# A decoder layer's Mamba mixer: its output kept channel-major, two heads per array pass, z as stationary weights

## The chip, the cores and the metric

The kernel runs on one core of a Trainium2 chip. The metric is device time in microseconds of one launch, the median of three runs; the profile is one further execution of the same program. TensorE multiplies (PE for the products, PEld for the loads of their stationary operand), VectorE (DVE), ScalarE (ACT) and GpSimd (POOL) do the element-wise work, and SyncE (SP) issues most transfers. Each engine takes its instructions strictly in program order; semaphores hold an instruction until its operands are there.

## The reference, cut to what matters

A trunk of two layers over 256 tokens of width 2048: a Mamba-2 layer, a gated feed-forward network, a shared K/V projection, an attention layer, and a second feed-forward network. The change lies in the Mamba-2 mixer alone (batch 1, 64 heads of 64 channels, 8 groups of 512 channels, state 128, two chunks of 128 tokens):

```python
def mamba2_mixer(x, w_in, conv_w, conv_b, dt_bias, a_log, d_skip, norm_w, w_out):
    zxbcdt = x @ w_in
    z, xbc, dt = ...                      # 4096, 4096 + 2*8*128, 64 columns
    xbc = silu(causal_dwconv(xbc, conv_w, conv_b))
    xs, b_ssm, c_ssm = ...
    dt = softplus(dt + dt_bias)
    a = -exp(a_log)
    y = ssd_chunked(xs * dt[..., None], a * dt, b_ssm, c_ssm)
    y = y + d_skip[:, None] * xs
    y = y.reshape(Bsz, S, D_INNER) * silu(z)
    yg = y.reshape(Bsz, S, N_SSM_GROUPS, D_INNER // N_SSM_GROUPS)
    yg = yg * rsqrt(mean(square(yg), axis=-1, keepdims=True) + RMS_EPS)
    return (yg.reshape(Bsz, S, D_INNER) * norm_w) @ w_out

def ssd_chunked(xdt, adt, b, c):          # chunks of l = 128 tokens
    a_cum = cumsum(a, axis=2)
    decay_in = exp(where(causal, a_cum[l] - a_cum[s], -inf))
    cb = einsum('bclgn,bcsgn->bclsg', c, b)
    y_diag = einsum('bclsgr,bcsgrp->bclgrp', cb[..., None] * decay_in, x)
    decay_to_end = exp(a_cum[:, :, -1:] - a_cum)
    chunk_states = einsum('bclgn,bclgr,bclgrp->bcgrpn', b, decay_to_end, x)
    ...                                   # prev: the state before each chunk
    y_off = einsum('bclgn,bcgrpn,bclgr->bclgrp', c, prev, exp(a_cum))
    return y_diag + y_off
```

With two chunks only the second has a state before it, so the kernel works `y_off` out once per group, as a product of the 128 x 128 block C2·B1 (`bc`) with the first chunk's scaled inputs (`xe`).

## The kernel before

**Weights as a stream of steps.** Every large product is cut into chunks of 512 weight columns (`chunks`, L59) and these into steps of 512 KB (`cut`, L81), 882 in all. A step's weights are loaded into a `raw` tile by SP (`load`, L162, four buffers), and `split` (L172) makes of them a rounded part `hi` (ACT, L183) and a remainder `lo` (DVE, L184). The activations are kept the same way, as `hi` and `lo` in `hT` (the layer's input, transposed), `yT` (the mixer's output, transposed) and others. A product is then the sum of three in the format fp32r: hi·hi, hi·lo and lo·hi. `splits` (L188) writes the split of step i+3 into the middle of step i, with four `hi` and four `lo` buffers, so weights are split up to three steps ahead; ACT can write a `hi` buffer only when TensorE has finished the step that used it four steps before.

**Two ways to multiply.** In mode "X" (`half`, L196) the activations are stationary and 512 weight columns stream past: 12 products of 128 x 512 a step (L206, L207, L211), and the result has tokens on the partitions. In mode "W" (`whole`, L225) the weights are stationary and the activations stream: 8 products of 128 x 512 (`hi` weights, both parts of the activations at once, L243) and 8 of 128 x 256 (`lo` weights, L245) a step, and the result has channels on the partitions, in two halves that are summed on the way out (`gather`, L546: a copy on ACT, an addition on DVE). An odd step of a mode-W chunk takes its `lo` products first (L233).

**What stands around the products.** `products(i)` writes step i; the functions registered with `at(i, f)` are written right behind it (L1059 to L1062). So the order of all engines' work is fixed by these step numbers. Accumulators come from `acc_pair` (three pairs of PSUM banks in turn), everything else that TensorE writes from `tp_tile` (two banks in turn).

**A group of the mixer.** For each of the 8 groups there are 8 steps for x (mode W) and 8 for z (mode X), 16 in all; `s0` is the first. In this text "step 7" of a group is s0+7, and what is planned at s0+16 and later stands in the next group's steps 0 and up. By step, in the plan at L775 to L797:
- 3: `m_load` fetches the group's cumulated decays, for all 8 heads, broadcast over the partitions (`mA`, two tiles, POOL's queue).
- 6: `m_cb` multiplies B and C (L673, L674; plain float32, which the trace shows as two passes each), DVE masks the result (`cb`, L676), ACT copies `bc` (L680). 6 to 8: `m_decay` (DVE, L685, L686) and `m_exp` (ACT, L690) make exp(a_cum[l] - a_cum[s]).
- 4 and 8: the gathers of x; 5 and 9: the four taps of the convolution (`taps`, L570: ACT L573, DVE L578). 12: `x_silu`. 13, 14: `m_mask` (DVE, L694) multiplies `cb` in.
- 15: `x_turn` transposes x to token-major (8 transposes, L708) and ACT copies it out (L709). 16: `x_dt` scales by dt and D (DVE, L716 to L719); `z_silu` (ACT).
- 18 and 19: `y_off` (one float32 product of 128 x 512, L732) and `y_diag` (8 float32 products a chunk, each with one head's 128 x 128 decay block stationary and its 64 channels moving, L724); DVE adds them up (L727, L734, L735).
- 21 to 23: `z_gate` (DVE, L744; ACT squares and sums, L747), `z_rms` (DVE L751, POOL L752), `z_scale` (DVE, L757).
- 28, 29: `z_turn` transposes the result back to channel-major, 4 transposes each (L340), and writes `yT` as `hi` (ACT, L763) and `lo` (DVE, L765).

Before the groups, `dt_turn` (L643) turns the per-head rows of dt, a_cum and their exponentials into `aux`. After them the product with `mamba_w_out` (mode X) reads `yT`.

Of the kernel before, what the change touches and what calls it, by code (L numbers as in the profile page):

```python
# [24 lines left out]
P = 128  # L25
# [16 lines left out]
NEG = -1.0e30  # L42


COL_AT, N_COL = {}, 0
for _name, _n in (("cw", 4 * CONV), ("cb", CONV), ("nw", DI), ("fw0", 6 * DFF), ("fcb0", 2 * DFF), ("fw1", 6 * DFF),
                  ("fcb1", 2 * DFF), ("dtb", P), ("alog", P), ("d", NH * P)):
    COL_AT[_name] = N_COL
    N_COL += _n // P
# [9 lines left out]
def chunks():  # L59
# [14 lines left out]
    for g in range(NG):  # L74
        out += some("W", "mamba_w_in", 0, DI + g * NC, 1, KD) + some("X", "mamba_w_in", 0, z + g * NC, 1, KD)
# [15 lines left out]
def yoco_kernel(ctx: ExitStack, tc: tile.TileContext, x, lmg, lmb, lfg, lfb, x_t, columns, w, out):  # L91
# [22 lines left out]
    cols = base.tile([P, N_COL], F32, name="cols")  # L114

    def load_cols():
        nc.sync.dma_start(cols, columns)
# [424 lines left out]
    d_bc = cols[:, COL_AT["d"]:COL_AT["d"] + NH]  # L542
    acum_d = dram.tile([NH, S], F32, name="acum_d")
    aux = mp.tile([P, 6, NH], F32, name="aux")
# [52 lines left out]
    def dt_exp():  # L597

        an = T["an"] = mp.tile([NH, 1], F32, name="an")
# [31 lines left out]
    def dt_cum():  # L631
# [9 lines left out]
        nc.scalar.activation(ex[:, P:], ac[:, P:], AF.Exp)  # L641

    def dt_turn():  # L643
        u, e, q, r, dt, ac, ex = T["t"]
        pt = tp_tile()
        for i, (t, c) in enumerate(((dt, 0), (dt, 1), (ac, 0), (ac, 1), (ex, 0), (ex, 1))):
            nc.tensor.transpose(pt[:, i * NH:(i + 1) * NH], t[:, c * P:(c + 1) * P], ident[:NH, :NH])
        nc.vector.tensor_copy(aux, pt[:, :6 * NH].rearrange("p (a h) -> p a h", h=NH))
# [38 lines left out]

    def m_exp(g, c):
# [14 lines left out]
    def x_turn(g):  # L703
        G[g]["xs"] = xs = t4k("xs")
        for h in range(2):
            ps = tp_tile()
            for i in range(4):
                nc.tensor.transpose(ps[:, i * P:(i + 1) * P], G[g]["xc"][:, i, h * P:(h + 1) * P], ident)  # L708
            nc.scalar.copy(xs[:, h], ps)  # L709

    def x_dt(g):
        xs = G[g]["xs"]
        G[g]["xdt"] = xd = t4k("xdt")
        G[g]["xe"] = xe = mp.tile([P, NC], F32, tag="xe", name="xe", bufs=1)
        for h in range(2):
            nc.vector.tensor_mul(heads(xd[:, h]), heads(xs[:, h]), hd(aux[:, h], g))  # L716
        nc.vector.tensor_mul(heads(xe), heads(xd[:, 0]), hd(aux[:, 4], g))
        for h in range(2):
            nc.vector.tensor_mul(heads(xs[:, h]), heads(xs[:, h]), hd(d_bc, g))  # L719

    def y_diag(g, c):
        ps = tp_tile()
        for h in range(8):
            nc.tensor.matmul(ps[:, h * 64:(h + 1) * 64], G[g]["A", c][:, h, :],  # L724
                             G[g]["xdt"][:, c, h * 64:(h + 1) * 64], start=True, stop=True)
        y = G[g]["xs"]
# [373 lines left out]
```

## Time and profile before

| what | value |
|---|---|
| median of three runs | 2558.22 us (2558.15 to 2558.3) |
| the profiled execution's own time | 2558.33 us |
| its span, first to last instruction | 2556.4 us |
| granted TensorE clock, mean | 0.999 |
| one group of the mixer, in the steady part | 51.02 us |
| the eight groups, from 154 to 563 us | 409 us, of which DVE 313 busy, ACT 228 |

A row of the timeline is: start, duration of the whole row, engine, line, operation, what it writes and reads, shape, how many in a row, and in brackets the idle time before it with what ended it. Durations of TensorE's products are modelled and overlap, so its pace is read from one start to the next. A row of the waits is: who waited for whom, the total, how often, the longest. A row of the chain in order of time is: start, duration, what. A row of the groups is: line, engine, operation, shape and count, then busy time and mean duration in ns.

### The profile page before, as it was taken

What the parts mean: (1) busy time and instruction counts of PE and PEld (TensorE: products, weight loads), DVE (VectorE), ACT (ScalarE), POOL (GpSimd) and SP (SyncE); (2) the same over time, 40 slices, a digit from 0 to 9 for tenths busy, and PEclk for the clock granted to TensorE, in tenths of its full rate; (3) what the DMA queues carried; (4) which work ended last, traced back from release to release, by engine and by line L of the source; (5) the groups of instructions that cost most, each with busy time, mean ns of one, the idle gap of its engine ahead of it and who ended that gap; (6) DMA issues with size and microseconds to landing.
All of it is one profiled execution on the core that took longest, in us unless ns stands there. A gap on an engine that the chain in (4) does not pass through costs nothing.

```text
span 2556.4 us, 35404 instructions
## 1 busy us (share of the span) xinstructions
PE 2543.6 (99%) x13744; PEld 2199.0 (86%) x13744; DVE 1666.5 (65%) x2138; ACT 1300.0 (51%) x1634; POOL 72.3 (3%) x87
## 2 busy tenths in 40 slices
PE   9999999999999999999999999999999999999998
PEld 8888888888888888888888888888888888888887
DVE  6877788854676666666444745655777676765545
ACT  6656556633465555555333444543555555554333
POOL 0000000000200000000000200000200000000001
PEclk9999999999999999999999999999999999999999
DMA  7555555557566565666676655456665666566675
GB/s 260 197 186 188 189 179 186 192 186 234 185 228 190 187 190 184 194 192 190 199 229 199 222 190 173 157 173 223 222 197 187 192 186 192 185 195 200 198 224 163
DMA packets 141495, 500.98 MB, mean 196 GB/s; under 512 B 15616, under 2 KB 16128, under 8 KB 141328
## 3 DMA queue, kind: packets, MB, share of 16 engines
q1 hardware_dynamic: 136976, 483.46, 58.8%
q0 software_dynamic: 4064, 14.75, 1.8%
q8 instruction: 107, 1.75, 0.3%
q14 instruction: 60, 0.49, 0.1%
q10 hardware_dynamic: 288, 0.52, 0.1%
HBM read 490.22 MB, written 8.45 MB: 195 GB/s over the span
## 4 chain that ended last, share of the span: by engine, by line
PE 98%; DVE 1%; issue 0%; ACT 0%; DMA 0%; SPq 0%; DVEq 0%
PE acc L243 36%; PE acc L245 19%; PE acc L211 13%; PE acc L206 13%; PE acc L207 13%; PE tp L724 1%; PE tp L211 0%; PE tp L207 0%; PE tp L206 0%; DVE lo L184 0%; PE tp L340 0%; PE tp L708 0%; PE tp L965 0%; PE tp L732 0%; DVE r L417 0%
## 5 line engine op out<-in xcount | busy, mean ns | idle before, releaser
L184 DVE TENSOR_TENSOR lo<-raw,hi 128x1024 fp32r<-128x1024 f32 (+1 forms) x871 | 1063.2, 1226 | 732.2 <-ACT hi L183 728.3
L183 ACT CAST hi<-raw 128x1024 fp32r<-128x1024 f32 (+1 forms) x871 | 912.6, 1049 | 915.6 <-PE acc L211 377.4
L243 PE MATMUL acc<-hT,hi 128*128 128x512 f32 x3984 | 961.4, 392 | 0.4 <-ACT hi L183 0.4
L243 PEld LDWEIGHTS acc<-hT,hi 128*128 128x128 f32 x3984 | 731.0, 188 | 141.7 <-ACT hi L183 1.0
L245 PEld LDWEIGHTS acc<-hT,lo 128*128 128x128 f32 x3984 | 512.5, 191 | 20.0
L245 PE MATMUL acc<-hT,lo 128*128 128x256 f32 x3984 | 522.5, 283 | 0.0
L207 PE MATMUL acc<-lo,gT 128*128 128x512 f32 (+1 forms) x678 | 254.5, 378 | 0.0
L206 PE MATMUL acc<-hi,gT 128*128 128x512 f32 (+1 forms) x678 | 254.1, 377 | 0.0
L211 PE MATMUL acc<-hi,gT 128*128 128x512 f32 (+1 forms) x678 | 200.8, 377 | 0.0
L206 PE MATMUL acc<-hi,hT 128*128 128x512 f32 x448 | 179.9, 402 | 0.0
L207 PE MATMUL acc<-lo,hT 128*128 128x512 f32 x448 | 175.2, 391 | 0.0
L207 PEld LDWEIGHTS acc<-lo,gT 128*128 128x128 f32 x678 | 127.7, 188 | 23.4
L206 PEld LDWEIGHTS acc<-hi,gT 128*128 128x128 f32 x678 | 127.5, 188 | 23.0
L211 PEld LDWEIGHTS acc<-hi,gT 128*128 128x128 f32 x678 | 124.9, 188 | 23.7
L211 PE MATMUL acc<-hi,hT 128*128 128x512 f32 x448 | 139.4, 392 | 0.6 <-DVE hT L353 0.6
L211 PEld LDWEIGHTS acc<-hi,hT 128*128 128x128 f32 x448 | 83.4, 188 | 20.5 <-DVE hT L353 3.0
L206 PEld LDWEIGHTS acc<-hi,hT 128*128 128x128 f32 x448 | 84.2, 188 | 17.2 <-ACT hT L352 1.3
L206 PE MATMUL acc<-hi,yT 128*128 128x512 f32 (+1 forms) x270 | 98.9, 371 | 0.0
L207 PEld LDWEIGHTS acc<-lo,hT 128*128 128x128 f32 x448 | 84.3, 188 | 16.9 <-DVE lo L184 0.9
L207 PE MATMUL acc<-lo,yT 128*128 128x512 f32 (+1 forms) x270 | 98.6, 369 | 0.0
L211 PE MATMUL acc<-hi,yT 128*128 128x512 f32 (+1 forms) x270 | 77.7, 369 | 0.0
L578 DVE SCALAR_TENSOR_TENSOR g<-u,cols,g 128x254 f32<-128x254 f32 (+1 forms) x176 | 73.5, 478 | 5.3 <-ACT g L573 5.3
(200 smaller groups left out, 1875.6 us busy)
## 6 DMA issues: line engine op xcount, KB each, us to landing
raw<-in_w SPq DMA_DIRECT2D x881, 512.0 KB, 4.1
mA<-acum_d POOLq DMA_DIRECT2D x16, 512.0 KB, 5.2
hres<-r POOLq DMA_DIRECT2D x12, 512.0 KB, 6.3
r<-hres SPq DMA_DIRECT2D x12, 512.0 KB, 5.1
r<-in_x SPq DMA_DIRECT2D x4, 512.0 KB, 5.2
gb<-in_ln_mix_g SPq DMA_DIRECT2D x8, 256.0 KB, 6.0
gb<-in_ln_mix_b SPq DMA_DIRECT2D x8, 256.0 KB, 6.4
gb<-in_ln_ffn_g SPq DMA_DIRECT2D x8, 256.0 KB, 5.5
```

What stands on the lines that cost most here:

```text
L183: nc.scalar.copy(h[:, sl], t[:, sl])
L184: nc.vector.tensor_sub(l[:, sl], t[:, sl], h[:, sl].bitcast(F32))
L206: nc.tensor.matmul(a, th, h[:, kk, sl], start=k == 0, stop=False)
L207: nc.tensor.matmul(a, th, l[:, kk, sl], start=False, stop=False)
L211: nc.tensor.matmul(a, ch.x.lo(k)[:, ts], h[:, kk, sl], start=False, stop=k == ch.nk - 1)
L243: nc.tensor.matmul(banks[j], h[:, kk, js], ch.x.both(k), start=begins, stop=ends, skip_group_check=True)
L245: nc.tensor.matmul(banks[j][:, :S], l[:, kk, js], ch.x.hi(k), start=begins, stop=ends, skip_group_check=True)
L578: nc.vector.scalar_tensor_tensor(d, u[:, i % 2, :S - k], c1(self.at_w, w[n - 1 - k] + self.ia + i), d, op0=OP.mult, op1=OP.add)
L724: nc.tensor.matmul(ps[:, h * 64:(h + 1) * 64], G[g]["A", c][:, h, :], G[g]["xdt"][:, c, h * 64:(h + 1) * 64], start=True, stop=True)
```

## The change

Channels stay on the partitions from the convolution to `yT`:
- z is computed in mode W like x, so it arrives as channels by tokens, in two halves, and is gathered, then put through silu (`z_silu`, by halves at steps 12 and 16).
- `y_diag` has the moving and the stationary operand exchanged: a head's 64 columns of `xdt` are stationary, its 128 x 128 decay block moves, and two heads go to the two halves of the array's columns (`tile_position`); the 16 products of a group write one accumulator pair. `y_off` becomes four products, with `xe` stationary and `bc` moving. The second chunk's decay factor exp(a_cum) is taken from `mA` (`m_into`, two exponentials on 64 partitions each, ACT) instead of from `aux`.
- D·x is a scaled copy in channel-major form (`y_d`, four on ACT).
- The squares are summed over the group's channels by two additions on DVE (`z_sum`) and two products with a column of 1/512 (`z_rms`); the root is spread over the partitions by a diagonal (`z_diag`, DVE) and one product with a matrix of ones (`z_scale`); then DVE multiplies and the `hi` and `lo` of `yT` follow. The transposes back (`z_turn`) go.
- TensorE's small float32 work stands at three places of a group, steps 6, 13 and 18 (= 2 of the next), instead of six: `z_rms` with `m_cb`, the preceding group's `z_scale` with `x_turn`, and `y_off` with `y_diag`.
- D is passed with one value per channel (32 columns instead of 64), and `cols`, `an` and the new `mean` are padded to a multiple of 64 floats.

```diff
+LINE = 64
...
-                  ("fcb1", 2 * DFF), ("dtb", P), ("alog", P), ("d", NH * P)):
+                  ("fcb1", 2 * DFF), ("dtb", P), ("alog", P), ("d", DI)):
...
     for g in range(NG):
-        out += some("W", "mamba_w_in", 0, DI + g * NC, 1, KD) + some("X", "mamba_w_in", 0, z + g * NC, 1, KD)
+        out += some("W", "mamba_w_in", 0, DI + g * NC, 1, KD) + some("W", "mamba_w_in", 0, z + g * NC, 1, KD)
...
-    cols = base.tile([P, N_COL], F32, name="cols")
+    cols = base.tile([P, -(-N_COL // LINE) * LINE], F32, name="cols")
...
     def load_cols():
-        nc.sync.dma_start(cols, columns)
+        nc.sync.dma_start(cols[:, :N_COL], columns)
...
     def c1(name, j):
...
-    d_bc = cols[:, COL_AT["d"]:COL_AT["d"] + NH]
+    mean = base.tile([P, LINE], F32, name="mean")
+    nc.gpsimd.memset(mean, 1.0 / NC)
+    ones = base.tile([P, P], F32, name="ones")
+    nc.gpsimd.memset(ones, 1.0)
...
-    aux = mp.tile([P, 6, NH], F32, name="aux")
+    aux = mp.tile([P, 5, NH], F32, name="aux")
...
     def gather(ch, half, dst, scale=None):
...
     def dt_exp():
...
-        an = T["an"] = mp.tile([NH, 1], F32, name="an")
+        an = T["an"] = mp.tile([NH, LINE], F32, name="an")[:, :1]
...
-        nc.scalar.activation(ex[:, P:], ac[:, P:], AF.Exp)
...
     def dt_turn():
...
-        for i, (t, c) in enumerate(((dt, 0), (dt, 1), (ac, 0), (ac, 1), (ex, 0), (ex, 1))):
+        for i, (t, c) in enumerate(((dt, 0), (dt, 1), (ac, 0), (ac, 1), (ex, 0))):
...
-        nc.vector.tensor_copy(aux, pt[:, :6 * NH].rearrange("p (a h) -> p a h", h=NH))
+        nc.vector.tensor_copy(aux, pt[:, :5 * NH].rearrange("p (a h) -> p a h", h=NH))
...
     def bc_silu(dst, g0):
...
+    def m_into(g):
+        G[g]["eA"] = e = mp.tile([P, 4, P], F32, tag="eA", name="eA", bufs=1)
+        for q in range(2):
+            ps = slice(64 * q, 64 * q + 64)
+            nc.scalar.activation(e[ps], G[g]["A", 1][ps].rearrange("p (j q) l -> p j q l", q=2)[:, :, q, :], AF.Exp)
     def m_exp(g, c):
...
     def x_turn(g):
-        G[g]["xs"] = xs = t4k("xs")
-        for h in range(2):
-            ps = tp_tile()
-            for i in range(4):
-                nc.tensor.transpose(ps[:, i * P:(i + 1) * P], G[g]["xc"][:, i, h * P:(h + 1) * P], ident)
-            nc.scalar.copy(xs[:, h], ps)
-    def x_dt(g):
-        xs = G[g]["xs"]
...
+        ps = acc_pair()
...
-            nc.vector.tensor_mul(heads(xd[:, h]), heads(xs[:, h]), hd(aux[:, h], g))
+            for i in range(4):
+                nc.tensor.transpose(ps[:, h, i * P:(i + 1) * P], G[g]["xc"][:, i, h * P:(h + 1) * P], ident)
+        for h in range(2):
+            nc.vector.tensor_mul(heads(xd[:, h]), heads(ps[:, h]), hd(aux[:, h], g))
...
+    def y_d(g):
+        G[g]["y"] = y = t4k("y").rearrange("p a (k t) -> p (a k) t", t=S)
+        for i in range(4):
+            nc.scalar.activation(y[:, i, :], G[g]["xc"][:, i, :], AF.Copy, scale=c1("d", 4 * g + i))
+    def y_diag(g):
+        ps = acc_pair()
+        for c in range(2):
+            for h in range(8):
+                j, q = divmod(h, 2)
+                nc.tensor.matmul(ps[64 * q:64 * q + 64, c, j * P:(j + 1) * P], G[g]["xdt"][:, c, h * 64:(h + 1) * 64],
+                                 G[g]["A", c][:, h, :], start=True, stop=True, tile_position=(0, 64 * q))
+        y = G[g]["y"].rearrange("p j (c l) -> p c j l", c=2)
+        nc.vector.tensor_add(y, y, ps.rearrange("p c (j l) -> p c j l", l=P))
+    def y_off(g):
+        ps = tp_tile()
+        for j in range(4):
+            nc.tensor.matmul(ps[:, j * P:(j + 1) * P], G[g]["xe"][:, j * P:(j + 1) * P], G[g]["bc"], start=True,
+                             stop=True)
+        e, y = G[g]["eA"], G[g]["y"][:, :, P:]
+        nc.vector.tensor_mul(e, e, ps.rearrange("p (j l) -> p j l", l=P))
+        nc.vector.tensor_add(y, y, e)
+    def z_silu(g, half):
+        if half == 0:
+            G[g]["sz"] = t4k("sz").rearrange("p a (k t) -> p (a k) t", t=S)
+        sz = G[g]["sz"][:, 2 * half:2 * half + 2, :]
+        gather(chZ[g], half, sz)
+        nc.scalar.activation(sz, sz, AF.Silu)
+    def z_gate(g):
+        y, sz = G[g]["y"], G[g]["sz"]
+        nc.vector.tensor_mul(y, y, sz)
+        nc.scalar.activation(sz, y, AF.Square)
+    def z_sum(g):
+        sz = G[g]["sz"]
+        nc.vector.tensor_add(sz[:, :2], sz[:, :2], sz[:, 2:])
+        nc.vector.tensor_add(sz[:, 0], sz[:, 0], sz[:, 1])
+    def z_rms(g):
+        ps = tp_tile()
...
-            nc.vector.tensor_mul(heads(xs[:, h]), heads(xs[:, h]), hd(d_bc, g))
-    def y_diag(g, c):
+            nc.tensor.matmul(ps[:, h:h + 1], G[g]["sz"][:, 0, h * P:(h + 1) * P], mean[:, :1], start=True, stop=True)
+        rr = mp.tile([P, 2, 1], F32, tag="rr", name="rr")
+        nc.vector.tensor_scalar(rr[:, :, 0], ps[:, :2], RMS_EPS, None, op0=OP.add)
+        nc.gpsimd.tensor_tensor(rr, rr, mhalf, op=OP.pow)
+        G[g]["rr"] = rr
+    def z_diag(g):
+        G[g]["rd"] = rd = mp.tile([P, 2, P], F32, tag="rd", name="rd", bufs=1)
+        for h in range(2):
+            nc.vector.tensor_scalar(rd[:, h], ident, G[g]["rr"][:, h, :], None, op0=OP.mult)
+    def z_scale(g):
...
-        for h in range(8):
-            nc.tensor.matmul(ps[:, h * 64:(h + 1) * 64], G[g]["A", c][:, h, :],
-                             G[g]["xdt"][:, c, h * 64:(h + 1) * 64], start=True, stop=True)
-        y = G[g]["xs"]
-        nc.vector.tensor_add(y[:, c], y[:, c], ps)
-    def y_off(g):
-        ps = tp_tile()
-        nc.tensor.matmul(ps, G[g]["bc"], G[g]["xe"], start=True, stop=True)
-        y, xe = G[g]["xs"], G[g]["xe"]
-        nc.vector.tensor_mul(heads(xe), heads(ps), hd(aux[:, 5], g))
-        nc.vector.tensor_add(y[:, 1], y[:, 1], xe)
-    def z_silu(g):
-        G[g]["sz"] = sz = t4k("sz")
-        for h in range(2):
-            nc.scalar.activation(sz[:, h], chZ[g].part[h], AF.Silu)
-    def z_gate(g):
-        y, sz = G[g]["xs"], G[g]["sz"]
-        nc.vector.tensor_mul(y, y, sz)
-        G[g]["ss"] = ss = mp.tile([P, 2, 1], F32, tag="ss", name="ss")
-        for h in range(2):
-            nc.scalar.activation(sz[:, h], y[:, h], AF.Square, accum_out=ss[:, h, :])
-    def z_rms(g):
-        G[g]["rr"] = rr = mp.tile([P, 2, 1], F32, tag="rr", name="rr")
-        nc.vector.tensor_scalar(rr, G[g]["ss"], 1.0 / NC, RMS_EPS, op0=OP.mult, op1=OP.add)
-        nc.gpsimd.tensor_tensor(rr, rr, mhalf, op=OP.pow)
-    def z_scale(g):
-        y = G[g]["xs"]
-        for h in range(2):
-            nc.vector.tensor_scalar(y[:, h], y[:, h], G[g]["rr"][:, h, :], None, op0=OP.mult)
-    def z_turn(g, p):
-        ps = turn_pair([G[g]["xs"]], p)
-        ks = [(4 * g + 2 * p + kk, ps[:, kk * S:(kk + 1) * S]) for kk in range(2)]
-        for k, s in ks:
-            nc.scalar.activation(yT[:, k, 0, :], s, AF.Identity, scale=c1("nw", k))
-        for k, s in ks:
-            nc.vector.scalar_tensor_tensor(yT[:, k, 1, :], s, c1("nw", k), yT[:, k, 0, :].bitcast(F32),
-                                           op0=OP.mult, op1=OP.subtract)
+        nc.tensor.matmul(ps[:, :S], ones, G[g]["rd"].rearrange("p h t -> p (h t)"), start=True, stop=True)
+        y = G[g]["y"]
+        for i in range(4):
+            nc.vector.scalar_tensor_tensor(y[:, i, :], y[:, i, :], c1("nw", 4 * g + i), ps[:, :S], op0=OP.mult,
+                                           op1=OP.mult)
+        hi, lo = (yT[:, 4 * g:4 * g + 4, a, :] for a in range(2))
+        nc.scalar.copy(hi, y)
+        nc.vector.tensor_sub(lo, y, hi.bitcast(F32))
...
         s0 = chX[g].first
...
+        at(s0 + 6, m_into, g)
...
         conv4(chX[g], 4 * g, lambda g=g: x_new(g), 0).plan()
-        at(s0 + 12, x_silu, g)
+        at(s0 + 11, x_silu, g)
...
-        at(s0 + 15, x_turn, g)
-        at(s0 + 16, x_dt, g)
-        at(s0 + 16, z_silu, g)
+        if g:
+            at(s0 + 13, z_scale, g - 1)
+        at(s0 + 13, x_turn, g)
+        at(s0 + 13, y_d, g)
+        for b in range(2):
+            at(chZ[g].ready(b), z_silu, g, b)
...
-        at(s0 + 18, y_diag, g, 0)
-        at(s0 + 19, y_diag, g, 1)
-        at(s0 + 21, z_gate, g)
+        at(s0 + 18, y_diag, g)
+        at(s0 + 20, z_gate, g)
+        at(s0 + 21, z_sum, g)
...
-        at(s0 + 23, z_scale, g)
-        at(s0 + 28, z_turn, g, 0)
-        at(s0 + 29, z_turn, g, 1)
+        at(s0 + 23, z_diag, g)
+    at(s0 + 26, z_scale, NG - 1)
...
     def chain(norm, nxt=None, after=None):
...
-    rows.append(_np.repeat(_np.asarray(inputs["mamba_d"])[0], P).reshape(NH, P))
+    rows.append(_np.repeat(_np.asarray(inputs["mamba_d"])[0], DI // NH).reshape(-1, P))
...
```

## The prediction

> **What bounds the kernel now.** I read the page's busy times and chain first, then who waits for whom on TensorE, then the pace of the products in order of time.
>
> ```profile
> span 2556.4 us, 35404 instructions
> ...
> PE 2543.6 (99%) x13744; PEld 2199.0 (86%) x13744; DVE 1666.5 (65%) x2138; ACT 1300.0 (51%) x1634; POOL 72.3 (3%) x87
> ...
> PE 98%; DVE 1%; issue 0%; ACT 0%; DMA 0%; SPq 0%; DVEq 0%
> ```
>
> ```profile
> PE tp L524 <- POOL ident masks.py:199: 1.4, 1, 1.4
> ...
> PE tp L999 <- DVE aT L1003: 0.3, 1, 0.3
> ```
>
> The first row of the waits is the warm-up, the last one 0.3 us: TensorE waits for nobody after the start. Every nanosecond that the change takes from TensorE's stream, or makes it wait, is a nanosecond of the total. The stretch that the change touches has this load:
>
> ```profile
> 154.00:563.00 409.00, 409.00 (x2201) 350.16 (x2199) 313.36 (x415) 228.49 (x306) 19.13 (x22) 1.00 0.57 185
> ```
>
> Per group that is DVE 39 and ACT 29 of 51 us: free on the average, but in bursts. TensorE's pace comes from the chain in order of time (first four rows) and from the timeline of one group:
>
> ```profile
> 253.92 3.65 PE acc L243 x16
> 304.94 3.65 PE acc L243 x16
> 746.00 3.65 PE acc L243 x16
> 751.57 3.65 PE acc L243 x16
> ```
>
> ```profile
> 309.38 1.02 PE L732 MATMUL tp<-xe,bc 128*128 128x512 f32 x2
> 310.24 1.89 PE L724 MATMUL tp<-xdt,mA 128*128 128x64 f32 x16
> 311.94 1.20 PE L245 MATMUL acc<-hT,lo 128*128 128x256 f32 x8
> ...
> 314.82 1.90 PE L724 MATMUL tp<-xdt,mA 128*128 128x64 f32 x16
> 316.53 2.07 PE L243 MATMUL acc<-hT,hi 128*128 128x512 f32 x8
> ...
> 324.96 0.61 PE L673 MATMUL tp<-CT,BT 128*128 128x128 f32 x4
> ...
> 325.55 1.20 PE L245 MATMUL acc<-hT,lo 128*128 128x256 f32 x8
> ...
> 328.43 0.39 PE L206 MATMUL acc<-hi,hT 128*128 128x512 f32 x1
> ...
> 339.31 0.39 PE L206 MATMUL acc<-hi,hT 128*128 128x512 f32 x1
> ...
> 342.03 0.60 PE L340 MATMUL tp<-ident,xs 128*128 128x128 f32 x4
> 342.38 0.48 PE L206 MATMUL acc<-hi,hT 128*128 128x512 f32 x1
> 342.70 0.40 PE L207 MATMUL acc<-lo,hT 128*128 128x512 f32 x1
> ...
> 351.16 1.03 PE L708 MATMUL tp<-ident,xc 128*128 128x128 f32 x8
> 351.95 2.10 PE L243 MATMUL acc<-hT,hi 128*128 128x512 f32 x8
> ```
>
> A group lasts 304.94 - 253.92 = 51.02 us. A run of 16 L243 begins once in two steps of mode W, so such a step takes (751.57 - 746.00) / 2 = 2.78; four steps of mode X go from 328.43 to 339.31, 2.72 each. From start to next start the float32 clusters take 2.56 (`y_off` 0.86 and half of `y_diag` 1.70), 1.71, 0.59 (`m_cb`), 0.35 twice (`z_turn`) and 0.79 (`x_turn`): 6.35. Then 51.02 - 8 x 2.78 - 8 x 2.72 - 6.35 = 0.67 is left, 0.11 for entering and leaving each of six clusters.
>
> **The change on TensorE, part by part, us a group.**
> - z in mode W: 8 x (2.78 - 2.72) = +0.50.
> - `y_diag`: before, 32 passes in 3.41, 0.107 each, 64 columns moving behind a load of 128. After, 32 passes of 128 moving columns behind a load of 64. The transposes price a pass of 128 columns at 0.79 / 8, about 0.10, so I keep 0.107. If the two halves of the array work at the same time, 16 x 0.107 = 1.71 (-1.70); one after the other, 3.42 (0). No row shows two halves. I take -1.70, since consecutive heads sit in different halves and write different partitions; the other end stays for the range.
> - `y_off` as four products: 8 passes x 0.107 = 0.86, as before: 0.
> - `z_turn` away: -0.70. `z_rms`: two products of two passes, each paid by its load of 128: +0.43. `z_scale`: 256 columns, half of L732's 512: +0.43.
> - Three clusters fewer: -0.33. One transpose fewer in `dt_turn`: 0.06 once, left out.
>
> Sum -1.37, times eight: -11.0 us.
>
> **Loads and products.** How the halves can fail is seen from the loads:
>
> ```profile
> L724 PEld LDWEIGHTS tp<-xdt,mA 128*128 128x128 f32 x240 | 29.1, 192 | 4.0 <-issue 1.9 <-ACT hi L183 1.4
> ```
>
> A load here lasts 192 ns at one per 107 ns, so loads do run behind products that use the same rows. The Trainium skill speaks against that: "TensorE: Matmul & The Clock Gate", Part 3, The mechanism, lets a load overlap a running product only where the row groups differ, and "TensorEngine Tiling (Array Packing)", Key Properties, adds that a change of tiling mode drains the array. The trace contradicts the first for the undivided array and cannot show the second; what both would make of the time is the third rival.
>
> **The change on DVE and ACT.** The accumulators' order (six pairs a group on three places) leaves each place's reader two steps or more; POOL and SP get no more transfers, and `mA` is free a step earlier. So this work costs nothing as long as the split weights come in time. They are what is late next. The tightest stretch before, on DVE and then ACT:
>
> ```profile
> 323.98 2.55 DVE L578 SCALAR_TENSOR_TENSOR xc<-u,cols,xc 128x255 f32<-128x255 f32 x6 [1.89 <-ACT xc L573]
> ...
> 327.65 0.41 DVE L676 TENSOR_TENSOR cb<-tp,tri 128x256 f32<-128x256 f32 x1
> 327.99 1.21 DVE L685 TENSOR_TENSOR mA<-mA,aux 128x1024 f32<-128x1024 f32 x1
> 329.24 0.69 DVE L686 TENSOR_SCALAR mA<-mA 128x1024 f32<-128x1024 f32 x1
> 329.84 1.22 DVE L184 TENSOR_TENSOR lo<-raw,hi 128x1024 fp32r<-128x1024 f32 x1
> 330.98 0.88 DVE L757 TENSOR_SCALAR xs<-xs,rr 128x512 f32<-128x512 f32 x2
> 331.77 1.22 DVE L685 TENSOR_TENSOR mA<-mA,aux 128x1024 f32<-128x1024 f32 x1
> ...
> 337.41 2.45 DVE L578 SCALAR_TENSOR_TENSOR xc<-u,cols,xc 128x255 f32<-128x255 f32 x6
> 339.77 3.49 DVE L184 TENSOR_TENSOR lo<-raw,hi 128x1024 fp32r<-128x1024 f32 x3
> ```
>
> ```profile
> 328.10 0.27 ACT L680 COPY bc<-tp 128x128 f32<-128x128 f32 x1 [2.73 <-DVE cb L676]
> 328.26 1.05 ACT L183 CAST hi<-raw 128x1024 fp32r<-128x1024 f32 x1
> 329.33 1.28 ACT L690 ACT_TABLE_LOAD   x1
> ```
>
> *Step 6.* `z_sum` (two additions, about 1.1) falls into the 1.89 that DVE idled ahead of the taps. But ACT now has the table load and the two exponentials of `m_into` between `bc` and the next `hi`: 1.28 + 2 x 0.55 (512 elements, half of an `m_exp`; bounds 0.5 and 0.6) = 2.4. That `hi` ends at 331.7 instead of 329.3, while DVE, free at 329.84, stands with its `lo` at the head of the queue: 1.86 lost. `z_diag` (two of 128 columns, about 0.2 each) instead of the scaling (0.79) gives 0.4 back. All that follows comes 1.46 later: the `lo` for step 13, the first of the three at 339.77, ends at 340.99 + 1.46 = 342.45. Before, it was needed at 342.70; without the first `z_turn`, and with 2.78 a step, step 13 starts at 325.55 + 6 x 2.78 = 342.23, and it is odd, so it takes `lo` first. A wait of about 0.3.
>
> *Step 13.* Behind it DVE makes the `lo` of 14 to 16 and half a gather of z between ACT's copies, `x_silu` and silu: from 342.4, `lo` 14 to 343.5, 15 after ACT's `x_silu` and `hi` to 345.2, the addition to 345.8, 16 after silu and `hi` to 348.6; mask 349.75. Then comes the last group's normalization ahead of this group's x:
>
> ```profile
> L694 DVE TENSOR_TENSOR mA<-mA,cb 128x1024 f32<-128x1024 f32 x14 | 17.0, 1215 | 0.0
> L765 DVE SCALAR_TENSOR_TENSOR yT<-tp,cols,yT 128x256 fp32r<-128x256 f32 x32 | 14.0, 478 | 4.7 <-ACT yT L763 4.7
> L716 DVE TENSOR_TENSOR xdt<-xs,aux 128x512 f32<-128x512 f32 x14 | 9.0, 684 | 0.0
> ```
>
> Four multiplications like L765 (0.44 apart) to 351.5, ACT's copy of 1024 (1.05) to 352.6, the `lo` of `yT` (1.15) to 353.75, three scalings of x (0.6 apart) to 355.5, and only then the `lo` of step 17, to 356.7. ACT has `y_d` in the same time and is no earlier. TensorE: step 13 ends at 345.3, the cluster takes 0.43 + 0.79 + 0.11, three steps 8.35: step 17, odd, starts at 354.95. A wait of 1.75, and behind that `lo` the mask for `y_diag` and the next `lo` queue, which still come in time.
>
> So 8 x 0.3 + 7 x 1.75 (the first group has no normalization before it) = +14.7. Bounds: 0, if ACT and DVE run 2 us ahead of this reckoning; 24, at 3 a group. **Sum:** 2558.3 - 11.0 + 14.7 = 2562.0. 2558.33 is the profiled execution's own time, 1.9 outside its span and 0.1 above the median, which is nothing here.
>
> **The rivals.**
> 1. *No waits.* The chain above adds some twenty durations, and in its 14.3 us from step 13's `lo` to step 17's DVE waits for ACT three times, 3.2 us in all, which could go faster. For: before, TensorE never waited and the least lead was 342.70 - 340.99 = 1.71. Against: that lead is smaller than what is put into the queue. Then 2558.3 - 11.0 = 2547.3.
> 2. *One head after the other* (slower): the halves take turns, since one load path and one moving stream serve both. `y_diag` keeps 3.4 us, 13.6 in all: 2575.6 with the waits, 2560.9 without. It decides as soon as `y_diag` takes more than about 2.5 a group.
> 3. *Loads not hidden in the divided array*: each pass pays its load of 64 columns too, 0.054 (half of 0.107): 32 x 0.161 = 5.2, +3.5 a group against the forecast: 2590. What speaks against it is the row of the loads. This is the Trainium skill's rule from above.
> 4. *The padding moves the whole kernel* (faster): 16 L243 take 3.65, so 0.228 each, and 16 L245 the other 1.92, 0.120. That is 0.216 per 512 columns and 0.012 fixed per product, while L732's pass of 512 takes 0.43, twice 0.216, and nothing fixed. By the tiles' sizes `hT`, `hi`, `lo` start 32 bytes past a multiple of 64 before, and on one after; L732's operands lie on one already. If the fixed part came from that, about 12,900 products lose up to 155 us; half of it gives 2480. Against: those operands already lie alike among themselves, and a fixed part can have other causes.
>
> **How the numbers follow.** Forecast 0.32, rivals in order 0.26, 0.26, 0.06, 0.10. A difference under 0.2% (5.1 us) I count as no change, about what a measurement can tell. The forecast's own range is 2555 to 2570 and gives 0.03 faster, 0.14 the same, 0.15 slower; rival 1 and rival 4 are faster (rival 1 but for 0.01), rivals 2 and 3 slower (0.01 of rival 2 the same). Together, rounded: faster 0.38, same 0.15, slower 0.47. The range for 8 in 10 reaches from rival 1 less its spread, 2544, to rival 2 with its, 2580; rivals 3 and 4 stay out, 0.16.
>
> **What would show it.** `y_diag`'s 32 passes between two neighbours' starts: 1.7, 3.4 or 5.2. A group: 49.7 without waits, 51.7 with those reckoned. TensorE's waits for `lo`: at the starts of steps 13 and 17 (the latter step 1 of the next group), nowhere else; `lo` for step 17 behind the scalings of x. The `hi` behind `m_into` 2.4 later. Products outside the mixer at 2.78 a step as before; a faster pace there is rival 4. I am wrong if TensorE waits elsewhere, at `z_rms` for `z_sum` above all, or if the mixer alone doesn't account for the difference.

## The result, and the profile after

| | before | after |
|---|---|---|
| median | 2558.18 us (2557.98 to 2558.3) | 2581.28 us (2580.0 to 2583.36) |
| profiled execution, its span | 2558.33, 2556.4 | 2580.0, 2578.1 |
| granted TensorE clock, profiled execution | 0.999 | 0.997 |

The ratio is 1.0091, 95% interval 1.0074 to 1.0109: the change makes the kernel 23 us slower, 21.7 in the two profiled executions. The forecast was 2562.0 with a range of 2544 to 2580. The page of after, first the span and the busy times, then the chain by engine:

```profile
span 2578.1 us, 36030 instructions
...
PE 2545.9 (99%) x14031; PEld 2207.3 (86%) x14031; DVE 1680.7 (65%) x2154; ACT 1313.4 (51%) x1633; POOL 71.6 (3%) x89
...
PE 88%; DVE 6%; ACT 3%; issue 2%; DMA 0%; DVEq 0%; SPq 0%; ACTq 0%
```

TensorE, 98% of the chain before, now has 88%; VectorE and ScalarE hold 9%, though TensorE's busy time rose by 2.3 us only. The work isn't longer, it waits. For whom is in after's table of waits (who for whom, total, how often, longest):

```profile
PE acc L246 <- DVE lo L185: 15.9, 13, 2.2
PE tp L773 <- DVE sz L767: 1.7, 7, 0.2
...
PE acc L208 <- DVE lo L185: 1.1, 1, 1.1
PE acc L207 <- ACT hi L184: 0.6, 1, 0.6
```

Where the 21.7 us arise is seen from the first to the eighth group in the chain in order of time: `y_off` before,

```profile
156.49 0.86 PE tp L732 x2
...
513.48 0.86 PE tp L732 x2
```

and the `y_diag` behind it after:

```profile
157.09 1.90 PE acc L737 x32
210.78 1.90 PE acc L737 x32
264.47 1.90 PE acc L737 x32
319.75 1.90 PE acc L737 x32
...
537.28 1.90 PE acc L737 x32
```

Seven groups took 356.99 and take 380.19: +23.2, the rest of the span 1.5 less. A group lasts 53.7, and some (264.47 to 319.75) 55.3. The forecast was 51.7.

The three stretches on which the sum rested. TensorE at `y_off` and `y_diag`, timeline of after:

```profile
318.69 1.06 PE L746 MATMUL tp<-bc,xe 128*128 128x128 f32 x8
319.68 1.97 PE L737 MATMUL acc<-mA,xdt 128*64 128x128 f32 x32
321.57 1.21 PE L246 MATMUL acc<-hT,lo 128*128 128x256 f32 x8
```

The 32 passes of `y_diag` take 1.89 from start to next start; in the trace's records they begin in pairs 6 to 7 ns apart, one pair every 109 ns. The halves work at the same time. TensorE at the starts of steps 7 and 17 of one group:

```profile
225.33 1.20 PE L246 MATMUL acc<-hT,lo 128*128 128x256 f32 x8
...
257.75 1.22 PE L246 MATMUL acc<-hT,lo 128*128 128x256 f32 x8 [2.21 <-DVE lo L185]
```

Step 7 starts at 225.33 here and at 325.55 in the prediction's reckoning, so 100.22 is to be taken off its times. VectorE in between:

```profile
231.95 1.22 DVE L185 TENSOR_TENSOR lo<-raw,hi 128x1024 fp32r<-128x1024 f32 x1 [2.11 <-ACT hi L184]
...
241.54 2.35 DVE L185 TENSOR_TENSOR lo<-raw,hi 128x1024 fp32r<-128x1024 f32 x2
245.03 1.23 DVE L185 TENSOR_TENSOR lo<-raw,hi 128x1024 fp32r<-128x1024 f32 x1 [1.13 <-ACT hi L184]
...
250.77 1.65 DVE L790 SCALAR_TENSOR_TENSOR y<-y,cols,tp 128x256 f32<-128x256 f32 x4
...
254.68 1.28 DVE L722 TENSOR_TENSOR xdt<-acc,aux 128x512 f32<-128x512 f32 x2
...
256.48 1.22 DVE L185 TENSOR_TENSOR lo<-raw,hi 128x1024 fp32r<-128x1024 f32 x1
```

and ScalarE in the same time:

```profile
228.28 1.28 ACT L696 ACT_TABLE_LOAD   x1
229.57 1.27 ACT L696 ACTIVATE eA<-mA 64x512 f32<-64x512 f32 x2
230.87 1.05 ACT L184 CAST hi<-raw 128x1024 fp32r<-128x1024 f32 x1
...
241.71 1.28 ACT L711 ACT_TABLE_LOAD   x1 [0.81 <-DVE xc L582]
...
243.96 1.03 ACT L184 CAST hi<-raw 128x1024 fp32r<-128x1024 f32 x1
```

`m_into` holds the next `hi` up as reckoned, and VectorE stands 2.11 for it (1.86 was said). The normalization and the scaling of x do stand ahead of step 17's `lo` (256.48). But that `lo` starts where it was to end (356.7 - 100.22 = 256.48), 1.2 late. Nearly half of this is there when step 13's `lo` starts, at 241.54. The rest is added by step 15's `lo` at 245.03, which waits for ScalarE: there a table load of 1.28, ahead of `x_silu` and the next `hi`, starts only when the taps are done, at 241.71.

Third, the clock. Windows of after: us, then busy times, TensorE's first, then the granted clock (third from the right). Three windows have half of it, each behind a wait at step 17; the first row shows a window at another such wait, and the second the window right ahead of the first slow one:

```profile
254.02:257.43 3.41, 1.52 (x11) 1.24 (x9) 3.41 (x5) 3.41 (x6) 0.00 (x0) 1.00 0.00 0
...
308.63:312.04 3.41, 1.20 (x11) 1.00 (x10) 3.41 (x5) 3.41 (x5) 0.00 (x0) 1.00 0.00 0
312.05:315.46 3.41, 3.41 (x13) 2.82 (x12) 3.35 (x4) 0.09 (x2) 0.00 (x0) 0.50 0.68 198
...
366.66:370.07 3.41, 3.35 (x12) 3.06 (x13) 3.41 (x5) 0.73 (x2) 0.00 (x0) 0.50 0.52 161
...
475.89:479.30 3.41, 3.41 (x13) 3.02 (x13) 3.41 (x4) 0.38 (x1) 0.00 (x0) 0.50 0.61 183
```

After three of the six waits at step 17, and after no other, some ten products run at half pace.

### The profile page after: what moved, and what is told of

Its sections match the earlier page's. It is cut to its first block, busy times and chain, and to the rows that moved or that the text cites. A ratio compares the mean times of both kernels' runs of the same rounds, so it can differ in the third digit from the quotient of the medians.

```text
span 2578.1 us, 36030 instructions
## 1 busy us (share of the span) xinstructions
PE 2545.9 (99%) x14031; PEld 2207.3 (86%) x14031; DVE 1680.7 (65%) x2154; ACT 1313.4 (51%) x1633; POOL 71.6 (3%) x89
## 4 chain that ended last, share of the span: by engine, by line
PE 88%; DVE 6%; ACT 3%; issue 2%; DMA 0%; DVEq 0%; SPq 0%; ACTq 0%
PE acc L244 35%; PE acc L246 18%; PE acc L208 11%; PE acc L212 11%; PE acc L207 11%; DVE lo L185 2%; ACT hi L184 2%; PE acc L737 1%; DVE xc L582 1%; DVE y L790 0%; PE tp L212 0%; PE tp L208 0%; PE tp L207 0%; DVE y L761 0%; DVE yT L794 0%
## 5 line engine op out<-in xcount | busy, mean ns | idle before, releaser
L244 PE MATMUL acc<-hT,hi 128*128 128x512 f32 x4496 | 1084.3, 392 | 0.4 <-ACT hi L184 0.4
L244 PEld LDWEIGHTS acc<-hT,hi 128*128 128x128 f32 x4496 | 827.5, 189 | 160.8 <-ACT hi L184 1.0
L246 PEld LDWEIGHTS acc<-hT,lo 128*128 128x128 f32 x4496 | 580.7, 191 | 43.1 <-DVE lo L185 18.6
L246 PE MATMUL acc<-hT,lo 128*128 128x256 f32 x4496 | 595.5, 284 | 15.9 <-DVE lo L185 15.9
L208 PEld LDWEIGHTS acc<-lo,gT 128*128 128x128 f32 x678 | 127.6, 188 | 23.2
L555 DVE TENSOR_TENSOR u<-u,acc 128x512 f32<-128x512 f32 x108 | 73.5, 681 | 16.4 <-ACT u L554 16.4
L207 PE MATMUL acc<-hi,hT 128*128 128x512 f32 x192 | 78.8, 410 | 0.0
L208 PE MATMUL acc<-lo,hT 128*128 128x512 f32 x192 | 75.5, 393 | 0.0
L582 DVE SCALAR_TENSOR_TENSOR v<-u,cols,v 128x254 f32<-128x254 f32 (+1 forms) x176 | 73.1, 478 | 0.0
L946 ACT CAST gT<-v 128x512 fp32r<-128x512 f32 x44 | 27.3, 620 | 84.5 <-DVE v L945 84.5
L554 ACT COPY u<-acc 128x512 f32<-128x512 f32 x108 | 62.1, 576 | 0.0
```

Of the source, the lines that this page charges most:

```text
L207: nc.tensor.matmul(a, th, h[:, kk, sl], start=k == 0, stop=False)
L208: nc.tensor.matmul(a, th, l[:, kk, sl], start=False, stop=False)
L244: nc.tensor.matmul(banks[j], h[:, kk, js], ch.x.both(k), start=begins, stop=ends, skip_group_check=True)
L246: nc.tensor.matmul(banks[j][:, :S], l[:, kk, js], ch.x.hi(k), start=begins, stop=ends, skip_group_check=True)
L554: nc.scalar.copy(dst, p[:, :, S:])
L555: nc.vector.tensor_add(dst, dst, p[:, :, :S])
```

## The experiments

The theory after the result: TensorE's stream is shorter as forecast, and all the loss is waits for work queued on VectorE and ScalarE, plus a clock that the longest of these waits lets fall. Rivals: the stream itself is longer (halves that share, loads that aren't hidden), or something outside the mixer. All ratios below are to the kernel before.

**The clock.** The kernel after with twelve transposes of the identity, which nobody reads, put into the wait of step 17:

```diff
+    def keep_warm(g):
+        ps = tp_tile()
+        for i in range(12):
+            nc.tensor.transpose(ps[:, (i % 4) * P:(i % 4 + 1) * P], ident, ident)
...
+        at(s0 + 16, keep_warm, g)
```

> The changed kernel with 12 transposes of the identity, read by nobody, put behind step 16 of each group, right ahead of the step at which TensorE waits 2.4 us for a split weight. In the changed kernel's trace three of these waits are followed by some ten products at half their pace (427 instead of 227 ns), 1.6 us each. Theory 'the clock falls because TensorE stands idle too long': the 12 transposes (1.3 us) lie inside the wait, 1.1 us of idling are left, no stretch at half pace follows, granted clock back to 0.999, and the time falls by 4 to 8 us, to about 2575, although work was added. Rival 'the slow stretch belongs to the late weight itself, for instance two engines at the same buffer': the stretches stay and the time stays at 2580 or above.

2576.3 us (2576.16 to 2576.38), ratio 1.0071 [1.0057, 1.0084]. Its table of waits, and its clock behind the same wait:

```profile
PE acc L246 <- DVE lo L185: 8.0, 13, 0.9
```

```profile
366.90:370.40 3.50, 3.50 (x20) 3.01 (x19) 3.47 (x4) 0.20 (x1) 0.00 (x0) 1.00 0.61 207
```

TensorE does 96 transposes more, its steps keep their distances, and the kernel is 5 us faster, since nothing runs at half pace; the executions now agree within 0.2 us instead of 3.4. That is the clock's share of the loss, and the reason for after's spread. With four transposes instead of twelve:

> The changed kernel with 4 transposes of the identity behind step 16 instead of 12. They take 0.45 us of the wait, so TensorE idles about 1.9 us at step 17, between the 1.5 us that left the pace alone in the run with m_into at step 7 and the 2.4 us of the changed kernel, where three of six waits were followed by a stretch at half pace. Theory 'it is the length of the idle time against a window': fewer half-pace stretches than in the changed kernel or none, 2576 to 2579, with the runs closer together than the 3.4 us of the changed kernel. Rival 'any product in between does it': as with 12, 2576.3.

2578.68 us (2576.87 to 2581.91), 1.0082 [1.0068, 1.0096], between the two, with executions further apart than after's, where closer ones were expected. In its profile one of six waits is followed by half pace, behind 1.77 us of idleness:

```profile
419.06 1.95 PE L246 MATMUL acc<-hT,lo 128*128 128x256 f32 x8 [1.77 <-DVE lo L185]
```

Why three of after's six waits lower the clock, though all six last 2.21 us, can be read off its windows above. The slow stretches start at 312.05, 366.66 and 475.89, that is 54.61 and 109.23 apart: 16 and 32 times their own length of 3.413. Counted on in such steps, the stretch ahead of each slow one holds nearly the whole wait, and TensorE is busy in it for 1.20, 1.26 and 1.20. The other three waits are cut in two by a border between stretches, and no stretch there has less than 1.52 busy. So the clock of a stretch seems to follow from how busy TensorE was in the one before. No sharp limit comes out of this: with four transposes the clock fell after a stretch with 1.64 busy, and not after another with 1.65.

**What makes the `lo` late.** `m_into` alone moved one step on:

```diff
-        at(s0 + 6, m_into, g)
+        at(s0 + 7, m_into, g)
```

> The changed kernel with m_into at step 7 instead of 6, so that ACT makes the next hi ahead of the table load and the two exponentials. Theory 'the order on ACT makes DVE idle 2.1 us at step 6 and all lo after it late': that idle time goes, the lo of steps 10 to 17 end 1.2 to 1.7 us earlier, the waits at step 11 (0.08) and step 13 (0.55) go, the one at step 17 falls from 2.4 to about 1.3 us and no half-pace stretch follows it; about 1.7 us a group less, 2564 to 2567 in all. Rival 'DVE is the bound in this stretch by its amount of work': the idle time only moves and the time stays within 3 us of 2580.

2564.08 us (2563.29 to 2564.47), 1.0022 [1.0013, 1.0031], as expected: 17 us of the 23 come back.

```profile
PE acc L246 <- DVE lo L185: 8.2, 6, 1.4
```

The seven waits at step 13 are gone, the six at step 17 are down from 2.2 to 1.4, and the clock stays up. So one placement on ScalarE costs three things: the waits at step 13, a part of those at step 17, and the clock. The sum had the first two, too small, and not the third.

The scaling of x and `y_d` moved behind the `lo` of step 17 instead (x stays in its accumulators until step 15):

```diff
...
-        at(s0 + 13, y_d, g)
+        at(s0 + 15, x_dt, g)
+        at(s0 + 15, y_d, g)
```

> The changed kernel with the three scalings of x (DVE) and the four scaled copies y_d (ACT) at step 15 instead of 13, behind the split of step 17's weights. Theory 'step 17 waits because the normalization of the last group and the scalings of this one stand ahead of its lo on DVE, and y_d ahead of its hi on ACT': the lo of step 17 ends 1.8 us earlier, the wait falls from 2.4 to about 0.6 us, no half-pace stretch follows; steps 11, 13 and z_rms wait as before. About 2563. Rival 'the wait moves to the next step': a wait of over 1 us turns up at steps 18 to 20 and the time stays above 2572.

2567.89 us (2567.38 to 2568.11), 1.0038 [1.0025, 1.0051]: 5 us more than expected. The waits say why:

```profile
PE tp L776 <- DVE sz L770: 6.6, 8, 0.9
PE acc L246 <- DVE lo L185: 5.1, 13, 0.4
```

Step 17's wait fell to 0.4, but what left the queue ahead of it now stands ahead of `z_gate` and `z_sum`, and `z_rms` waits 0.9 a group instead of 0.2. Both moves together, and `z_gate` and `z_sum` a step earlier (19, 20):

```diff
-        at(s0 + 20, z_gate, g)
-        at(s0 + 21, z_sum, g)
+        at(s0 + 19, z_gate, g)
+        at(s0 + 20, z_sum, g)
```

> Both moves together, and z_gate and z_sum one step earlier (19 and 20) so that z_rms finds its sums. Theory 'the loss is waits and what follows them': TensorE waits nowhere in the mixer, and what is left is the change's own effect on its stream. By the terms of my sum a group then takes 49.65 us and the kernel 2547; by the difference that the changed kernel's trace shows between its group (53.7) and its waits (3.4) it takes 50.3 and the kernel 2552.5. Rival 'the changed stream is slower by itself': the kernel stays above 2560 with no waits.

**2554.21 us** (2553.76 to 2554.97), ratio 0.9985 [0.9976, 0.9994]: 0.15% faster than before and 27 us faster than after, with five entries of the plan moved. It is 1.7 us above the nearer of the two expectations and not quite without waits; it is called the kernel without waits below. Its waits and its first two `y_diag` in the chain:

```profile
PE acc L246 <- DVE lo L185: 2.3, 8, 0.4
```

```profile
157.30 1.90 PE acc L740 x32
207.25 1.90 PE acc L740 x32
```

The first groups are free of waits and take 49.95, 1.07 less than before: by this pace the change's own work on TensorE is a gain of 8 to 9 us. TensorE's products and their order are the same in after, so the 27 us between the two kernels are waits and clock.

**Further moves.** Against the waits that are left, the second chunk's decay and exponentials were moved later, to steps 10 and 11, and the first mask earlier, from 13 to 11:

```diff
-        at(s0 + 7, m_decay, g, 1)
-        at(s0 + 8, m_exp, g, 1)
+        at(s0 + 10, m_decay, g, 1)
+        at(s0 + 11, m_exp, g, 1)
-        at(s0 + 13, m_mask, g, 0)
+        at(s0 + 11, m_mask, g, 0)
```

> The version before (both moves, z_gate and z_sum a step earlier) still waited 0.57 us at step 17 and up to 0.3 at step 13 in most groups. Here, besides, the second chunk's m_decay and m_exp stand at steps 10 and 11 instead of 7 and 8, and the first chunk's mask at 11 instead of 13: ahead of the two tight places DVE has 1.9 and 1.1 us less to do, in gaps where it waited for ACT. Theory 'what is left above the stream are these waits': none is left in the mixer, the time falls by 4 to 6 us to 2548 to 2550, and the group shows what the change does to TensorE's stream alone. Rival 'the waits only move on': the time stays at 2553 or above.

2569.51 us (2568.72 to 2570.67), 1.0045 [1.0032, 1.0057]: 15 us worse. Its waits, and ScalarE ahead of `x_silu`:

```profile
PE acc L718 <- ACT xc L711: 9.0, 6, 1.5
PE acc L246 <- DVE lo L185: 6.7, 6, 1.3
```

```profile
346.30 1.06 ACT L700 ACTIVATE mA<-mA 128x1024 f32<-128x1024 f32 x1 [3.57 <-DVE mA L689]
...
348.67 1.06 ACT L711 ACTIVATE xc<-xc 128x1024 f32<-128x1024 f32 x1
```

ScalarE stands 3.57 us for the moved decay and only then comes to `x_silu`; `x_turn` waits for that, a wait that neither kernel had. The smaller step, both masks one step later (14, 15) in the kernel without waits:

> The kernel with all waits moved out (2554.2), and the two masks one step later (14 and 15), so that the first of them (1.14 on VectorE) stands no longer ahead of the normalization and the lo of step 17. The wait of 0.41 at step 17 should go: 7 x 0.4 = -2.8, 2551.4. If y_diag then waits for the second mask or for x's scaling instead, no gain: 2554 or more.

2554.48 us (2554.11 to 2555.01), 0.9986 [0.9977, 0.9994]: no gain.

```profile
PE acc L246 <- DVE lo L185: 1.7, 8, 0.2
...
PE tp L776 <- DVE sz L770: 0.3, 1, 0.3
```

Step 17's wait is gone as expected, but steps 11 and 13 now wait about 0.45 each (from start to start), and `z_rms` 0.2. A group stays at 51.1, and the wait has only changed its place.

What holds a group at 51.1 is seen in the chain of the kernel without waits (2554.21), one group apart:

```profile
354.47 3.91 DMA raw<-in_w
...
405.51 3.79 DMA raw<-in_w
```

In these 51.04 us the chain runs over one load of weights, ScalarE and VectorE, and TensorE isn't on it. The two variants below on the same plan begin with groups of 50.55 and 50.37 instead of 49.95, by their slower products, and they too come to 51.04 to 51.09, the last group apart. So TensorE has a lead in the first groups and then goes at the pace at which split weights come. This is read off the chain and the starts; no run shortened the chain itself.

**The two halves of the array.** The heads in the order 0, 2, 4, 6, 1, 3, 5, 7, so that neighbours share a half. First in the kernel with the decay moved, where it told little:

> The version without waits, with the heads of y_diag taken in the order 0, 2, 4, 6, 1, 3, 5, 7, so that neighbours lie in the same half of the array. Theory 'neighbours in different halves run at the same time, 32 passes in 1.75 us': now only one neighbouring pair a chunk differs, the 32 passes take about 3.4, and the time rises by 1.6 us a group, 12 to 13 in all. Rival 'the passes are short for another reason, for instance the load of 64 columns instead of 128': the cluster stays at 1.9 us and the time does not change.

2570.66 us (2570.23 to 2571.64), 1.0051 [1.0035, 1.0066], +1.15 to its own base, because the waits behind `y_diag` (x_turn's fell from 1.5 to 0.9) took up what it lost. Again in the kernel without waits:

```diff
-            for h in range(8):
+            for h in (0, 2, 4, 6, 1, 3, 5, 7):
```

> The kernel with all waits moved out (2554.2), but in y_diag the heads go 0, 2, 4, 6 to the one half of the array and then 1, 3, 5, 7 to the other, so that no two neighbours can run at once. If the halves share nothing, the cluster of y_diag takes 3.4 us instead of 1.89, +1.5 a group; there is hardly a wait after it that could take it up, so +12 in all: 2566. If a pass of 128 columns is bounded by something else than the half it runs in, nothing changes: 2554.

2555.62 us (2555.16 to 2556.79), 0.9991 [0.9982, 1.0]: +1.4, not +12. TensorE's timeline:

```profile
308.74 2.57 PE L740 MATMUL acc<-mA,xdt 128*64 128x128 f32 x32
311.23 1.21 PE L246 MATMUL acc<-hT,lo 128*128 128x256 f32 x8
```

`y_diag` takes 2.49 to the next start instead of 1.89, so +0.6 a group and not +1.5; the rest is taken up by the remaining waits. Neither theory expected that. In the records four passes run alone, 109 ns apart, and from the fifth on the other half's passes run beside them. The pass that signals the end of the first chunk is the 16th to start in the kernel without waits, and the 19th here: three passes of the next four heads have overtaken it.

**The padding.** Without it (`cols`, `an` and `mean` as long as they need to be), `hT` starts 32 bytes past a multiple of 64 and `hi` and `lo` on one; with it, and before the change, they start alike. These addresses are worked out from the tiles' sizes; no view shows them. In the kernel with the decay moved:

```diff
-    cols = base.tile([P, -(-N_COL // LINE) * LINE], F32, name="cols")
+    cols = base.tile([P, N_COL], F32, name="cols")
...
-    mean = base.tile([P, LINE], F32, name="mean")
+    mean = base.tile([P, 1], F32, name="mean")
...
-        an = T["an"] = mp.tile([NH, LINE], F32, name="an")[:, :1]
+        an = T["an"] = mp.tile([NH, 1], F32, name="an")
```

> The version without waits, with cols, an and mean not padded. By the sizes, hT then starts 32 bytes past a multiple of 64, and hi, lo, yT, gT on a multiple of 64: the activations and the weights lie unlike each other, where before and after they lie alike (both 32 past, both on a multiple). Theory 'addresses do not matter to the products', as 227 and 120 ns a product before and after at different addresses suggest: the products keep these intervals and the time stays within 2 us. Rival 'likeness matters': products of an activation with a weight take longer, by the 7 or 13 ns that their intervals have over 213 and 107, which over some 12,900 products is 80 us or more.

2584.42 us (2584.18 to 2586.13), 1.0105 [1.0091, 1.0118], 14.9 more than with it, between the 2 and the 80 of the two expectations. The same edit in the kernel without waits:

> The kernel with all waits moved out (2554.2), without the padding, so that hT starts 32 bytes past a multiple of 64 and hi and lo on one. If unlike addresses cost 5 to 8 ns a product of 512 columns, as seen in the run without padding before, about 15 us more than with it: 2569. If that run lost its time to something else, 2554.

2569.87 us (2569.42 to 2570.39), 1.0046 [1.0032, 1.006], 15.7 more. Its products far from the mixer:

```profile
758.86 2.05 PE L246 MATMUL acc<-hT,lo 128*128 128x256 f32 x16
760.75 3.89 PE L244 MATMUL acc<-hT,hi 128*128 128x512 f32 x16
764.48 2.06 PE L246 MATMUL acc<-hT,lo 128*128 128x256 f32 x16
...
770.11 2.05 PE L246 MATMUL acc<-hT,lo 128*128 128x256 f32 x16
```

Four steps take 770.11 - 758.86 = 11.25, 2.81 each instead of 2.78. And the kernel before with the padding, so that all of them start on a multiple of 64:

> The kernel before, with cols and an padded, so that hT, hi, lo and yT all start on a multiple of 64 instead of 32 bytes past one; nothing else differs. The rival of the padding, with half of the fixed part of a product gained: 2480. If only likeness matters, 512 columns keep 227 ns and 256 keep 120: 2558.

2557.59 us (2556.92 to 2558.84), 0.9998 [0.9989, 1.0008]: nothing.

```profile
755.50 2.08 PE L246 MATMUL acc<-hT,lo 128*128 128x256 f32 x16
...
772.20 2.08 PE L246 MATMUL acc<-hT,lo 128*128 128x256 f32 x16
```

Six steps in 16.70, 2.78 each as ever. In the three layouts that were run, it counts whether the operands start alike and not where; the fourth, `hT` on a multiple of 64 and the weights 32 bytes past one, wasn't run.

## Why the prediction was wrong

The direction (slower had been given 0.47), the places of the two long waits and the order of work that makes them were right. The sizes were not: +3.7 was said, +21.7 came, 18.0 more. From the starts of TensorE's products in after, group by group against the 49.95 us group without waits, us over the seven groups and the rest of the span:

| term | forecast | measured | how |
|---|---|---|---|
| TensorE's own stream | -11.0 | -8.8 | 7 x 49.95 - 356.99 = -7.3, and the -1.5 outside |
| wait, step 17 | +12.25 | +16.9 | six of 2.47, the last group's in all 2.1 |
| wait, step 13 | +2.4 | +4.5 | 7 x 0.64 |
| wait, `z_rms` | 0 | +3.3 | 7 x 0.47 |
| wait, step 11 | 0 | +1.3 | 7 x 0.18 |
| clock after step 17's wait | 0 | +4.7 | 1.59 + 1.50 + 1.58 |
| sum | +3.7 | +21.9 | 21.7 by the spans, the rest is rounding |

- **The step that failed** is the reckoning of VectorE's queue, waits of 14.7 where 26.0 came. Step 15's `lo` ended 1.2 later than reckoned (245.03 + 1.14 = 246.17, against 345.2 - 100.22 = 244.98), and all behind it, to step 17's `lo`, kept that delay. Nearly half of it, 0.53, is there at step 13, whose `lo` starts at 241.54 against 339.77 + 1.46 - 100.22 = 241.01: VectorE stood 2.11 for the `hi` behind `m_into` and not 1.86, and smaller delays came with that. The other 0.66 comes between the two, where 4.63 passed and not 3.97: ACT loads a table for 1.28 there, which "15 after ACT's `x_silu` and `hi` to 345.2" doesn't name. No run took that load away, so its share is read from the trace alone. "Nowhere else" was wrong too: `z_rms` waits for `z_sum`, which stood only among the things that would make the forecast wrong, and step 11 for a `lo` behind `m_into`. With `m_into` a step later the waits of 11 and 13 vanish together, which shows their common cause.
- **A wait costs more than its idle time.** The idle time of step 17 is 2.21, its cost 2.47; the product behind the first one comes 0.1 late again, as it does behind a float32 cluster. No term of the sum had that.
- **The clock** was no term at all: before, TensorE never stood long enough for it to show. It is 4.7 in the profiled execution, and 5.0 by the run with the twelve transposes.
- **TensorE's stream**: `z_turn` -0.72, `z_rms` +0.45, `z_scale` +0.44, as reckoned (-0.70, +0.43, +0.43). `y_off` and `y_diag` gain 1.39 instead of 1.70: the pairs come every 109 ns, and 0.2 us goes by between the last start ahead of the divided array and its first one, and again on the way out, twice the 0.107 of a pass. Three clusters fewer give 0.25, not 0.33. With z in mode W at +0.50, as reckoned, these come to -0.97 a group; 49.95 against 51.00 is -1.05, and 0.08 of that isn't assigned.
- **Rival 1** (no waits, 2547.3) doesn't describe the change, but with the waits moved out it nearly holds: 2554.2, the rest being the smaller stream gain, 2.2, and the waits that are left, 2.3 of idle time and 4.8 from start to start.
- **Rivals 2 and 3** fell on the starts in pairs and the 1.89 of `y_diag`; and even in the order made for it, rival 2's price would have been 0.6 a group, since TensorE reaches past the next products.
- **Rival 4** had the wrong sign of what is at stake: like addresses win nothing over like addresses, and unlike ones lose 16 us. In this change the padding keeps a loss away.

Open is from how much idle time in a stretch the clock falls, and what the chain of split weights would need to go below 51.04 a group. That step 17 waits in the same way for ScalarE's `y_d` wasn't tried apart from the scaling of x.

## What to carry to other kernels

Where an engine that sets the end has a margin of a microsecond or two, walk the queues of its suppliers instruction by instruction, table loads included, before placing new work; a share of busy time of 50 or 65% says nothing there. Moving one small step (`m_into`) was worth 17 of 23 us, and one move of the decay and the mask cost 15, so move work behind the instruction that is waited for, and look which wait is next. When several orders of the work all end at the same time a group, as here at 51.04 to 51.09, it is the suppliers' chain that has to become shorter. Price a wait of TensorE not by its idle time alone, but with the re-entry and, in these runs from 1.8 us on, the slow products that can follow.

## What the hardware showed unexpectedly

- **The clock falls after short idleness.** 2.21 us of idleness was followed by a granted clock of 0.50 and products of 427 ns instead of 227 for 3.41 us, in three of six cases; 1.77 in one of six; 1.5 and less in the runs above never. The Trainium skill, "TensorE: Matmul & The Clock Gate", Part 1, What's actually happening, says that the gate falls after an idle window of about 3.4 us and that the window runs freely. The half pace agrees, and so does the window that runs freely: the slow stretches start whole multiples of 3.413 us apart, and the waits that a border cut in two left the clock alone. A whole idle window doesn't agree: TensorE was busy for 1.20 to 1.26 us, and once for 1.64, of the 3.41 ahead of a slow stretch.
- **Products overtake.** With four heads in one half and then four in the other, passes of the later heads start beside the earlier ones, and three of them before the first chunk's last pass. The same page of the Trainium skill, Part 3, The mechanism, says that products start and end strictly in program order; for two halves of the array's columns the trace shows otherwise. The sentence at the start, that each engine takes its instructions strictly in program order, doesn't hold for these products either.
- **Unlike start addresses cost 1% of a mode-W step.** With `hT` 32 bytes past a multiple of 64 and the weights on one, 16 products of 512 columns take 3.73 instead of 3.65, 233 ns each instead of 228; 256 columns come a little faster, every 118 ns instead of 120. The padded kernel before shows that the common start itself doesn't matter.
